# Hybrid retention and attention block: two query splits and two first output loads placed earlier, a key's lower part placed behind the scores

## The chip, the cores and the metric

The kernel runs on 1 core of one Trainium2 chip. The metric is device time in microseconds of one execution. The kernel before took 1036.93 us in the median of 3 runs (1036.6 to 1037.95).

## The reference, cut to what matters

```python
u = rms_norm(h)                                  # 16 learned meta tokens ahead of 1024 positions
rq, rk, rv, rg, aq, ak, av, ag, gr, ga = split(u @ w_in)
o_r = group_norm(bidirectional_retention(rot(rq), rot(rk), rv)) * silu(rg)   # 4 heads
y_r = o_r @ w_ret_branch
o_a = windowed_sink_attention(rot(aq), rot(ak), av) * silu(ag)   # 8 heads, 2 key groups, 128-query blocks
y_a = o_a @ w_attn_branch
mix = sigmoid(gr) * y_r + sigmoid(ga) * y_a
out = h + rms_norm(mix @ w_out)                  # meta rows dropped
```

All of it is float32, with sequence 1024 and width 1024. In one block of the attention, 128 queries see a band of at most 384 keys, 16 meta keys, and a sink logit.

## The kernel before, in words

**Arithmetic.** Each float32 product is made of three passes of TensorE on operands of type float32r (`mm3`, L74 to L79): upper part by upper part (L76), lower by upper (L77), upper by lower (L78). So each operand is first split: the upper part is a rounded copy, made by ScalarE or GpSimd, and the lower part is the rest, a subtraction on VectorE (`dve_lo`, L92). A pass must wait for the part that it reads.

**Stages.** In order of time: projections and retention head by head (to 320 us), the last projection of that kind, the values of the attention (`gen_av`, nine chunks of 128 positions, to 330 us), the attention (to 545 us), and four phases of large products in Strassen's form, z (gates), r and a (branch projections) and o (output), to the end. In the attention and in the phases, TensorE's queue is filled so that some product always stands between a step and the next step that needs its result.

**The attention** goes through 32 chunks (hp, n): hp is a pair of heads, n a block of 128 queries. `stage1` makes the scores (`ps`) by TensorE from the keys `kTh`, `kTl` and the queries `aqh`, `aql`; VectorE adds the mask and takes the maximum (L1447), ScalarE the exponential (L1450), VectorE the reciprocal of its sum (L1454), GpSimd the scaling (`p`, L1463). `stage2` turns the weights by TensorE (`pt`, L1483, L1487, L1488) into two PSUM banks that serve two chunks by turns, and splits them into `pah`/`pal`, `pbh`/`pbl` and `pm`. A chunk's turning therefore needs its own `p` and a bank that `pal` (for L1483) and `pbl` (for L1487) of an earlier chunk have been read out of. `stage3` multiplies them by the values (`po`). Between the stages `fill` issues steps of other work: projections of later queries and keys, and partial products for later phases (`pe`).

The queries of a pair come out of a projection, are rotated (L187, L188 on VectorE, a DMA with addition from GpSimd's queue, L192), and are split by `split_q` into `aqh` (ScalarE, L678) and `aql` (VectorE), each half of the queries and each head of the pair by itself. The keys are split by `keys` into `kTh` (L724) and `kTl`. The table `BEGUN` says at which step of the fillings such a piece of work is issued.

The order on each engine is that of one list for each, made when the program is built; an engine does its list in order and waits at an instruction whose operands aren't there. `tc.issue_after(x)`, and `follow(...)` for several, put what stands inside them behind the instruction x in that order.

**The phases.** A product of a phase waits for its left operand's upper and lower part (`lh`, `ll`) and for its right operand's (`big` and `T`), and adds into a PSUM bank; `combine` reads the banks out (`u3`, `c1`, ...). The right operands of the next phase are loaded or split while the present one runs: `refill` gives the steps as a table of offsets to the end of the phase, `run` hooks them behind the products. For phase o, loaded in phase a, those are: pieces of `w_out` (`a`, L1246, 256 KB each) that are split into `big` (L963 on ScalarE, L92 on VectorE), and sums prepared long before (`preT`, L1142, 1 MB for each of upper and lower part). The left operands of phase o are tiles of the mixed activations, `wro` (512 KB, L1324), read from memory after the branch sums have been added there. All these loads are issued by SyncE in one list, in order.

**The names that the prediction uses:** `val` and `vah`: lower and upper part of the attention's values (L917, L918). `sto0S`, `sto1S`: left operands of phase o that are made from `wro` (L1009). `u3a` (L1077): a sum of phase a that VectorE reads out of the PSUM bank which TensorE's product 3 (`ba` with `lha`, L76) goes on to write.

Of the kernel before, what the change touches and what calls it, by code (L numbers as in the profile page):

```python
# [18 lines left out]
NB = SEQ // P  # L19
# [20 lines left out]
def block_kernel(ctx: ExitStack, tc: tile.TileContext, x0, xT, x, meta, w_in, w_rb, w_ab, w_out, post_w,  # L40
# [629 lines left out]
    def split_q(hp, e_, i):  # L670

        o = aq[hp][e_, i].rearrange("p (t q) -> p t q", q=64)
        if (hp, i) not in aqs:
            aqs[hp, i] = [aw.tile([P, 1024], R, tag=f"aq{t}", bufs=2, name=f"aq{t}{hp}_{i}") for t in "hl"], set()
            if len(aqs) == 1:
                aw.tile([P, 48], F32, name="space_aq")
        h, l = (t.rearrange("p (t e q) -> p t e q", e=2, q=64)[:, :, e_] for t in aqs[hp, i][0])
        nc.scalar.copy(h, o)  # L678
        dve_lo(l, o, h)
        aqs[hp, i][1].add(e_)  # L680


# [31 lines left out]

    rotated_k = {}

    def keys(g, i):

        if not i:
            kT[g] = [ra.tile([P, 4, 272], R, tag="kp", bufs=2, name=f"kT{s}{g}") for s in "hl"]  # L720
        kh, kl = kT[g]
        o = rotated_k.pop((g, i))
        s = NM if i == 0 else 0
        nc.scalar.copy(kh[:, i, 0:256], o[:, s:s + 256])  # L724
        dve_lo(kl[:, i, 0:256], o[:, s:s + 256], kh[:, i, 0:256])
        if i == 0:
            for j in range(4):
                nc.scalar.copy(kh[:, j, 256:272], o[:, 0:NM])
                dve_lo(kl[:, j, 256:272], o[:, 0:NM], kh[:, j, 256:272])
# [173 lines left out]
    def gen_av():  # L903
        w = load_w(w_in, U_AV)
        for c in range(9):
            mt = None if c else vmt
            t = projT(w, c, f"pav{c}", mt)
            if c == 0:
# [5 lines left out]
                for r in range(2):  # L914
                    nc.sync.dma_start(vm[32 * r + NM:32 * r + 2 * NM].bitcast(F32), mt)
            else:
                nc.scalar.activation(vah[:, c - 1], t[:, 0:256], AF.Copy, scale=rcol[:, c:c + 1])  # L917
                nc.vector.scalar_tensor_tensor(low_value(c - 1), t[:, 0:256], rcol[:, c:c + 1],  # L918
# [235 lines left out]
    def refill(nm, src):  # L1154
# [20 lines left out]
        def got(n):  # L1175
            return lambda: get_pre(n)

        def step(at, n, f):
            for k, j in enumerate(n):
                at.setdefault(j, []).append(lambda k=k: f(k))  # L1180

        if nm == "a":
            at = {-16: [load(0, 0)], -14: [load(1, 1)]}
            each(at, -13, split("B11", 0, 0))
            at.update({-11: [got("T1")], -10: [load(1, 0)], -9: [got("T2")], -5: [got("T3")], -1: [got("T4")]})
            each(at, -7, split("B21", 1, 0))
            each(at, -3, split("B22", 1, 1))
            return at

        first = -21 if nm == "z" else -17  # L1190
        at = {first: [load(0, 0), load(0, 1)], -13: [load(1, 1)], -9: [load(1, 0, range(3))]}
        def behind(f):
# [3 lines left out]
            return g  # L1196

        step(at, range(first + 2, first + 6), behind(minus((0, 1), (0, 1), (0, 0))))
        step(at, (-13, -12, -11, -10), split("B11", 0, 0))
# [12 lines left out]
    def run(phases):  # L1212
# [9 lines left out]
        for u in (0, 1):  # L1222
            hooks.setdefault(len(jobs) - len(ph_o.seq) - 11 + u, []).insert(0, lambda u=u: ph_o.block(u, "A11"))
        for k, at in enumerate((16, 27, 46, 58)):
# [98 lines left out]
    def o_load(t, u, j):  # L1323
        nc.sync.dma_start(t, mx_d[4 * j:4 * j + 4, :, 256 * (u ^ 2):256 * (u ^ 2) + 256].rearrange("k p t -> p k t"))  # L1324

# [84 lines left out]
    def attention():  # L1410
# [14 lines left out]
        def stage1(hp, n):  # L1425
# [10 lines left out]
            for x_ in range(2):  # L1436
# [10 lines left out]
                nc.vector.tensor_tensor_reduce(r[:, o:o + wid], s[:, 0:wid], seen, -SCALE,  # L1447
                                               nsink[:, hp:hp + 1], ALU.add, ALU.min, nm_[:, x_:x_ + 1])
# [86 lines left out]
        fill = filler([hooked(works, BEGUN)])[0]  # L1535

        with follow(*latest):
            fill(3)
        with follow(*latest):
            stage1(0, 0)  # L1540
        for k, (hp, n) in enumerate(chunks):
# [28 lines left out]
            if k in (12, 14, 21):  # L1570
# [139 lines left out]
```

## Time and profile before

| | us |
|---|---|
| median of 3 runs | 1036.93 |
| lowest, highest run | 1036.6, 1037.95 |
| the profiled execution, its own time | 1035.83 |
| its span (first to last instruction) | 1034.1 |
| TensorE busy in the span | 1022.3 (99%) |
| VectorE, ScalarE, GpSimd busy | 831.9, 502.0, 226.3 |
| mean granted TensorE clock | 0.998 |

The span is what the trace covers; 1.73 us of the execution's own time lie around it. TensorE is busy through nearly all of the span, so a change of a few microseconds can only be found in the few places where TensorE waits; the view of the waits lists them. In rows of the timeline, the columns are: start in us, duration in us, engine, line, operation, written tile, read tiles, shapes, count, and, in brackets, how long the engine had been idle and what released it. A matmul's duration contains the time it takes to pass through the array, in which the next one already runs: one of 512 columns lasts 0.39 us, and the next starts 0.23 us after it. Idle time of TensorE is therefore shown some 0.16 us shorter than the delay that it makes.

### The profile page before, as it was taken

How to read it: one execution, taken by the hardware profiler on the slowest of the kernel's cores; microseconds unless marked ns; L12 is line 12 of the kernel's file. 1: busy time of each engine (PE TensorE's matmuls, PEld its weight loads, DVE VectorE, ACT ScalarE, POOL GpSimd, SP SyncE). 2: the span in 40 equal slices, each digit the busy share in tenths (PEclk: the TensorE clock that was granted, in tenths of full speed). 3: DMA queues.
4: the chain of work that ended last, by engine and by line, in shares of the span. 5: the costliest groups of instructions: out<-in, count | busy, mean ns of one | idle time of the engine just before them, and what ended most of it. 6: DMA issues, size and time to landing. Idle time of an engine off the chain costs nothing. (4 is left out here: it accounts for less than half of the span.)

```text
span 1034.1 us, 17322 instructions
## 1 busy us (share of the span) xinstructions
PE 1022.3 (99%) x5883; PEld 898.8 (87%) x5883; DVE 831.9 (80%) x1802; ACT 502.0 (49%) x1129; POOL 226.3 (22%) x368
## 2 busy tenths in 40 slices
PE   9999999999999999999999999999999999999997
PEld 8998999989989888988888888888888888887886
DVE  7886759758876787777769999998989899777765
ACT  5531432523423466655667555455567456333442
POOL 3445244243341424443310000000000000110032
PEclk9999999999999999999999999999999999999999
DMA  9433123243241447666559589899874756889563
GB/s 360 164 87 88 63 46 87 76 78 112 80 97 62 103 152 206 184 183 174 154 171 347 178 287 330 312 319 319 276 265 141 257 196 200 246 216 330 139 122 81
DMA packets 98840, 188.45 MB, mean 182 GB/s; under 512 B 13024, under 2 KB 37632, under 8 KB 98192
## 3 DMA queue, kind: packets, MB, share of 16 engines
q1 hardware_dynamic: 81200, 162.89, 46.6%
q0 software_dynamic: 10176, 14.73, 9.5%
q10 hardware_dynamic: 7376, 9.73, 2.8%
q8 instruction: 46, 0.75, 0.3%
q14 instruction: 42, 0.34, 0.1%
HBM read 124.32 MB, written 57.68 MB: 176 GB/s over the span
## 5 line engine op out<-in xcount | busy, mean ns | idle before, releaser
L1310 POOL DMA_DIRECT2D mx_d<-c1a x4 | 3.6, 891 | 395.3 <-DMA a<-in_w_out_dram 368.6
L77 PE MATMUL bz<-big,llz 128*128 128x512 f32 x192 | 74.9, 390 | 0.5 <-DVE llz L92 0.5
L78 PE MATMUL bz<-big,lhz 128*128 128x512 f32 x192 | 74.4, 389 | 0.0
L76 PE MATMUL bz<-big,lhz 128*128 128x512 f32 x192 | 74.1, 389 | 0.0
L76 PE MATMUL pv<-wh,big 128*128 128x256 f32 x256 | 72.9, 285 | 0.0
L77 PE MATMUL pv<-wh,big 128*128 128x256 f32 x256 | 72.8, 284 | 0.0
L78 PE MATMUL pv<-wl,big 128*128 128x256 f32 x256 | 72.7, 284 | 0.0
L78 PE MATMUL bz<-T,lhz 128*128 128x512 f32 x176 | 68.5, 389 | 0.0
L77 PE MATMUL bz<-T,llz 128*128 128x512 f32 x176 | 68.5, 389 | 0.0
L76 PE MATMUL bz<-T,lhz 128*128 128x512 f32 x176 | 68.2, 389 | 0.0
L1450 ACT ACTIVATE p<-raw,nm 128x337 f32<-128x337 f32 (+1 forms) x64 | 35.5, 557 | 34.1 <-DVE nm L1447 30.5
L76 PE MATMUL paq<-big,wh 128*128 128x512 f32 x128 | 51.6, 403 | 0.0
L1463 POOL TENSOR_SCALAR p<-p,den 128x336 f32<-128x336 f32 (+2 forms) x60 | 32.6, 565 | 85.9 <-DVE den L1454 81.1
L78 PE MATMUL paq<-big,wh 128*128 128x512 f32 x128 | 50.2, 392 | 0.0
L77 PE MATMUL paq<-big,wl 128*128 128x512 f32 x128 | 50.2, 392 | 0.0
L76 PEld LDWEIGHTS pv<-wh,big 128*128 128x128 f32 x256 | 48.4, 189 | 0.4
L77 PEld LDWEIGHTS pv<-wh,big 128*128 128x128 f32 x256 | 48.3, 189 | 0.4
L78 PEld LDWEIGHTS pv<-wl,big 128*128 128x128 f32 x256 | 48.3, 189 | 0.3
L92 DVE TENSOR_TENSOR wl<-wr,wh 128x1024 fp32r<-128x1024 f32 x28 | 35.1, 1258 | 11.3 <-POOL wh L89 6.7
L77 PEld LDWEIGHTS bz<-big,llz 128*128 128x128 f32 x192 | 36.1, 188 | 8.1 <-DVE llz L92 0.8
L78 PEld LDWEIGHTS bz<-big,lhz 128*128 128x128 f32 x192 | 36.0, 188 | 7.5
L76 PEld LDWEIGHTS bz<-big,lhz 128*128 128x128 f32 x192 | 36.1, 188 | 7.5
(621 smaller groups left out, 3591.2 us busy)
## 6 DMA issues: line engine op xcount, KB each, us to landing
wrz<-in_w_in_dram SPq DMA_DIRECT2D x32, 512.0 KB, 6.0
wr<-in_w_in_dram SPq DMA_DIRECT2D x29, 512.0 KB, 4.0
we<-in_w_in_dram SPq DMA_DIRECT2D x16, 512.0 KB, 4.2
tg<-tg_d SPq DMA_DIRECT2D x32, 256.0 KB, 5.3
e<-e ACTq DMA_DIRECT2D x20, 256.0 KB, 2.4
e<-e SPq DMA_DIRECT2D x20, 256.0 KB, 4.6
xn<-in_x_dram SPq DMA_DIRECT2D x8, 512.0 KB, 9.4
oTr_d<-ost SPq DMA_DIRECT2D x16, 256.0 KB, 2.1
```

The source lines that it names most:

```text
L76: nc.tensor.matmul(o, ah, bh, start=first, stop=False, **kw)
L77: nc.tensor.matmul(o, al, bh, start=False, stop=False, **kw)
L78: latest[:] = [nc.tensor.matmul(o, ah, bl, start=False, stop=last, **kw).ins]
L92: return nc.vector.tensor_tensor(o, i, hi.bitcast(F32), ALU.subtract).ins
L1310: nc.gpsimd.dma_start(d, to, accum_op=ALU.add)
L1450: last["exp"] = nc.scalar.activation(pp[:, x_, w0 - o:w0 - o + 1 + wid], r[:, 0:1 + wid], AF.Exp, scale=-1.0, bias=nm_[:, x_:x_ + 1], accu ...
L1463: nc.gpsimd.tensor_scalar(v, v, den[:, x_:x_ + 1], 1.0, op0=ALU.mult, op1=ALU.mult)
```

## The change

Four places are changed.

**First queries' splits ahead of the last values.** `gen_av` stops once more, before the read-out of its last chunk, and `split_q` of the first pair's first half (both heads) is issued ahead of it; the last read-out follows the two upper parts. The old place was in `stage1` of the first chunk. On ScalarE, where these are the last read-outs of the values, before:

```order
L917 ACTIVATE vah<-pav_4826,rcol 128x256
L609 ACTIVATE ost_2_4856<-to_2_4853,rnw 128x128 x2
L609 ACTIVATE ost_2_4856<-to_1_4859,rnw 128x128 x2
L917 ACTIVATE vah<-pav_4865,rcol 128x256
L678 CAST aqh_0_4931<-aq_00_4507 128x8x64
L678 CAST aqh_0_4931<-aq_01_4563 128x8x64
```

and after:

```order
L924 ACTIVATE vah<-pav_4826,rcol 128x256
L609 ACTIVATE ost_2_4856<-to_2_4853,rnw 128x128 x2
L609 ACTIVATE ost_2_4856<-to_1_4859,rnw 128x128 x2
L678 CAST aqh_0_4913<-aq_00_4507 128x8x64
L678 CAST aqh_0_4913<-aq_01_4563 128x8x64
L924 ACTIVATE vah<-pav_4865,rcol 128x256
```

The two upper parts of the queries have passed the last chunk's `vah`. On VectorE the last `val` goes, in the same way, from ahead of the preparing memsets and the two `aql` to behind the second `aql`.

**A keys' lower part behind the scores.** `keys(1, 2)` makes the upper part at its old place, and leaves the lower part to the next `stage1`, behind its two score instructions. On VectorE, in chunk (2, 2), before:

```order
L92 TENSOR_TENSOR wl_0_6450<-wr_0_6272,wh_0_6449 128x1024
L92 TENSOR_TENSOR kTl_6223<-akr_2_6374,kTh_6222 128x256
L187 TENSOR_TENSOR m_aq_11_6460<-paq_11_6380,sr 128x512
L188 TENSOR_TENSOR aq_11_6459<-paq_11_6380,cr 128x512
L1447 ISA raw_0_6321,nm_2_6479<-ps_2_0_6481,mask,nsink 128x336
L1447 ISA nm_2_6479 128x1
L1447 ISA raw_1_6329,nm_2_6479<-ps_2_1_6487,mask,nsink 128x336
L1447 ISA nm_2_6479 128x1
L1454 RECIPROCAL den_2_6480<-den_2_6480 128x2
```

and after:

```order
L92 TENSOR_TENSOR wl_0_6449<-wr_0_6272,wh_0_6448 128x1024
L187 TENSOR_TENSOR m_aq_11_6459<-paq_11_6380,sr 128x512
L188 TENSOR_TENSOR aq_11_6458<-paq_11_6380,cr 128x512
L1461 ISA raw_0_6321,nm_2_6478<-ps_2_0_6480,mask,nsink 128x336
L1461 ISA nm_2_6478 128x1
L1461 ISA raw_1_6329,nm_2_6478<-ps_2_1_6486,mask,nsink 128x336
L1461 ISA nm_2_6478 128x1
L92 TENSOR_TENSOR kTl_6223<-akr_2_6374,kTh_6222 128x256
L1471 RECIPROCAL den_2_6479<-den_2_6479 128x2
```

The subtraction `kTl` has gone from ahead of the rotation and the scores to behind them, ahead of the reciprocal.

**A queries' split ahead of a turning.** `split_q(3, 1, 1)` is taken out of the table (step 172) and issued in chunk (3, 2) ahead of `stage2`. On ScalarE `aqh` goes from behind `pah`, `pm`, `pbh` to ahead of them; on VectorE `aql` from behind `pal`, `pm`, `pbl` to ahead of them, right behind the reciprocal.

**First output loads in one row.** The two first `wro` tiles are asked for at one hook (offset -11) ahead of the sums `T1`, which now follow the second of them in SyncE's list; the splits of `w_out`'s pieces are put behind the newest lower part of a left operand. In SyncE's list, before:

```order
L1292 DMA mr_11317<-mx_d 128x512
L1246 DMA a_11347<-in_w_out_dram 128x512
L1324 DMA wro_0_11311<-mx_d 128x4x256
L1142 DMA big_112<-preT_96 128x4x512
L1142 DMA big_113<-preT_97 128x4x512
L1324 DMA wro_0_11339<-mx_d 128x4x256
L1142 DMA T_7800<-preT_98 128x2048
```

and after:

```order
L1305 DMA mr_11319<-mx_d 128x512
L1337 DMA wro_0_11311<-mx_d 128x4x256
L1259 DMA a_11347<-in_w_out_dram 128x512
L1337 DMA wro_0_11313<-mx_d 128x4x256
L1149 DMA big_112<-preT_96 128x4x512
L1149 DMA big_113<-preT_97 128x4x512
L1149 DMA T_7800<-preT_98 128x2048
```

The second `wro` has passed the 2 MB of `preT`, and a last piece of `w_out` now stands behind the first `wro`. On VectorE, `sto1S`, which reads the second `wro`, goes up by two instructions, and some splits of `w_out` change places with neighbours; on TensorE one pass (L77 of `ba`, product 4) goes ahead of twelve passes of product 3.

The diff, cut to its core:

```diff
@@ split_q
-        nc.scalar.copy(h, o)
+        upper = nc.scalar.copy(h, o).ins
         dve_lo(l, o, h)
         aqs[hp, i][1].add(e_)
+        return upper
@@ keys
-    rotated_k = {}
-
-    def keys(g, i):
+    rotated_k, lowers = {}, []
+
+    def keys(g, i, apart=False):
...
-        dve_lo(kl[:, i, 0:256], o[:, s:s + 256], kh[:, i, 0:256])
+        lower = lambda: dve_lo(kl[:, i, 0:256], o[:, s:s + 256], kh[:, i, 0:256])
+        if apart:
+            lowers.append(lower)
+        else:
+            lower()
@@ gen_av
             else:
+                if c == NB:
+                    yield
                 nc.scalar.activation(vah[:, c - 1], t[:, 0:256], AF.Copy, scale=rcol[:, c:c + 1])
@@ refill
+        def got_behind(n):
+            def f():
+                with follow(*asked):
+                    get_pre(n)
+            return f
...
+        def behind(f):
+            def g(k):
+                with tc.issue_after(ahead[0]):
+                    f(k)
+            return g
         if nm == "a":
             at = {-16: [load(0, 0)], -14: [load(1, 1)]}
-            each(at, -13, split("B11", 0, 0))
-            at.update({-11: [got("T1")], -10: [load(1, 0)], -9: [got("T2")], -5: [got("T3")], -1: [got("T4")]})
-            each(at, -7, split("B21", 1, 0))
-            each(at, -3, split("B22", 1, 1))
+            each(at, -13, behind(split("B11", 0, 0)))
+            at.update({-11: [got_behind("T1")], -10: [load(1, 0)], -9: [got("T2")], -5: [got("T3")], -1: [got("T4")]})
+            each(at, -7, behind(split("B21", 1, 0)))
+            each(at, -3, behind(split("B22", 1, 1)))
             return at
@@ run
         for u in (0, 1):
-            hooks.setdefault(len(jobs) - len(ph_o.seq) - 11 + u, []).insert(0, lambda u=u: ph_o.block(u, "A11"))
+            hooks.setdefault(len(jobs) - len(ph_o.seq) - 11, []).insert(u, lambda u=u: ph_o.block(u, "A11"))
@@ o_load
-        nc.sync.dma_start(t, mx_d[4 * j:4 * j + 4, :, 256 * (u ^ 2):256 * (u ^ 2) + 256].rearrange("k p t -> p k t"))
+        asked[:] = [nc.sync.dma_start(
+            t, mx_d[4 * j:4 * j + 4, :, 256 * (u ^ 2):256 * (u ^ 2) + 256].rearrange("k p t -> p k t")).ins]
@@ stage1 of the attention
+            with tc.issue_after(scored):
+                while lowers:
+                    lowers.pop(0)()
             last["sum"] = nc.vector.reciprocal(den, den).ins
@@ the attention's loop
+        with follow(*[split_q(0, e_, 0) for e_ in range(2)]):
+            next(av, None)
         with follow(*latest):
             fill(3)
...
+            if chunks[k] == (3, 2):
+                with follow(*marks("exp", "sum")):
+                    split_q(3, 1, 1)
             with follow(*latest, *marks("exp", "sum")) if not ends else ExitStack():
                 stage2(hp, n)
@@ BEGUN
-             110: [(split_q, 2, 0, 1)], 116: [(keys, 1, 2)], 117: [(half_w, 'q', 3, 0)], 121: [(half_w, 'q', 3, 1)],
+             110: [(split_q, 2, 0, 1)], 116: [(keys, 1, 2, True)], 117: [(half_w, 'q', 3, 0)], 121: [(half_w, 'q', 3, 1)],
...
-             170: [(pre_parts, 11)], 171: [(pre_fetch, 12)], 172: [(split_q, 3, 1, 1)], 176: [(pre_sum, 12, 0)],
+             170: [(pre_parts, 11)], 171: [(pre_fetch, 12)], 176: [(pre_sum, 12, 0)],
```

More of the change, by code (lines that the diff above doesn't have):

```diff
@@ L1180, in step @@
                 at.setdefault(j, []).append(lambda k=k: f(k))
-        if nm == "a":
-            at = {-16: [load(0, 0)], -14: [load(1, 1)]}
-            each(at, -13, split("B11", 0, 0))
-            at.update({-11: [got("T1")], -10: [load(1, 0)], -9: [got("T2")], -5: [got("T3")], -1: [got("T4")]})
-            each(at, -7, split("B21", 1, 0))
-            each(at, -3, split("B22", 1, 1))
-            return at
-        first = -21 if nm == "z" else -17
-        at = {first: [load(0, 0), load(0, 1)], -13: [load(1, 1)], -9: [load(1, 0, range(3))]}
         def behind(f):
@@ L1196, in behind @@
             return g
+        if nm == "a":
+            at = {-16: [load(0, 0)], -14: [load(1, 1)]}
+            each(at, -13, behind(split("B11", 0, 0)))
+            at.update({-11: [got_behind("T1")], -10: [load(1, 0)], -9: [got("T2")], -5: [got("T3")], -1: [got("T4")]})
+            each(at, -7, behind(split("B21", 1, 0)))
+            each(at, -3, behind(split("B22", 1, 1)))
+            return at
+        first = -21 if nm == "z" else -17
+        at = {first: [load(0, 0), load(0, 1)], -13: [load(1, 1)], -9: [load(1, 0, range(3))]}
         step(at, range(first + 2, first + 6), behind(minus((0, 1), (0, 1), (0, 0))))
@@ L1446, in stage1 @@
                 o, w0 = (0, 64) if x_ else (1, 1)
-                nc.vector.tensor_tensor_reduce(r[:, o:o + wid], s[:, 0:wid], seen, -SCALE,
-                                               nsink[:, hp:hp + 1], ALU.add, ALU.min, nm_[:, x_:x_ + 1])
+                scored = nc.vector.tensor_tensor_reduce(r[:, o:o + wid], s[:, 0:wid], seen, -SCALE,
+                                                        nsink[:, hp:hp + 1], ALU.add, ALU.min, nm_[:, x_:x_ + 1]).ins
                 last["exp"] = nc.scalar.activation(pp[:, x_, w0 - o:w0 - o + 1 + wid], r[:, 0:1 + wid], AF.Exp,
```

## The prediction, made before the changed kernel had run

> **What bounds the kernel now.** I read the view of TensorE's waits first, since the page has TensorE busy in 99% of the span: a change can win only where TensorE stands still, and lose by making it stand still elsewhere.
>
> ```profile
> PE ps L77 <- DVE aql L92: 1.0, 2, 0.5
> PE ba L76 <- DVE u3a L1077: 0.6, 1, 0.6
> PE pt L1483 <- DVE pal L92: 0.5, 1, 0.5
> PE bz L77 <- DVE llz L92: 0.5, 1, 0.5
> PE pt L1487 <- DVE pbl L92: 0.4, 1, 0.4
> PE pt L1483 <- POOL p L1463: 0.2, 1, 0.2
> ```
>
> The columns are total, count and longest, in us. These are seven waits (but for the first matmul of the kernel), six of them for VectorE. The change touches five: both of the first row (places 1 and 3), the third and fifth (place 2), the second (place 4). It leaves the fourth and sixth alone. I then went through the timeline at each place.
>
> **Place 1, the first scores.**
>
> ```profile
> 327.11 1.14 ACT L609 ACTIVATE ost<-to,rnw 128x128 f32<-128x128 f32 x4
> ...
> 329.92 0.47 ACT L917 ACTIVATE vah<-pav,rcol 128x256 fp32r<-128x256 f32 x1 [1.68 <-PE pav L78]
> ...
> 330.30 1.13 ACT L678 CAST aqh<-aq 128x512 fp32r<-128x512 f32 x2
> ...
> 331.78 0.41 PE L76 MATMUL ps<-kTh,aqh 128*128 128x272 f32 x2
> ...
> 331.96 0.68 DVE L92 TENSOR_TENSOR aql<-aq,aqh 128x512 fp32r<-128x512 f32 x1
> 332.70 0.39 PE L77 MATMUL ps<-kTh,aql 128*128 128x272 f32 x1 [0.51 <-DVE aql L92]
> 332.93 0.29 PE L78 MATMUL ps<-kTl,aqh 128*128 128x272 f32 x1
> ```
>
> ScalarE stands idle 1.68 us, up to 329.92, with the two `aqh` queued behind the last `vah`. In the new order they start when `ost` ends, at 327.11 + 1.14 = 328.25, and end at 329.38, before `vah` can start; so `vah` loses nothing. Both `aql`, 0.68 each, can then be done by about 329.38 + 0.7 = 330.1 to 330.8 (the short memsets ahead of them fill VectorE's idle time). TensorE asks for them at 331.78 + 2 x 0.13 = 332.03 (a pass of 272 columns takes 0.13), so some 1.2 us are in hand, and the wait of 332.70 - 332.03 = 0.67 goes. The next pass starts 0.23 after the delayed one and not 0.13: a wait costs 0.10 more behind it. The last `val`, moved behind the `aql`, is still ready some 0.5 us ahead of the first score's masking, which is in turn behind TensorE. Sum of the place: **0.77**.
>
> **Place 2, the key's lower part.**
>
> ```profile
> 452.43 0.42 DVE L92 TENSOR_TENSOR kTl<-akr,kTh 128x256 fp32r<-128x256 f32 x1 [0.88 <-ACT kTh L724]
> ...
> 454.07 0.56 DVE L1447 CUSTOM_DVE_ANT_0 raw<-ps,mask,nsink 128x336 f32<-128x336 f32 x1
> ...
> 456.47 0.69 DVE L92 TENSOR_TENSOR pal<-pt,pah 128x512 fp32r<-128x512 f32 x1 [0.30 <-ACT pah L1493]
> 456.51 0.32 PE L78 MATMUL ps<-kTl,aqh 128*128 128x336 f32 x1
> ...
> 457.30 0.71 PE L1483 MATMUL pt<-ident,p 128*128 128x128 f32 x4 [0.47 <-DVE pal L92]
> ...
> 457.87 0.42 DVE L92 TENSOR_TENSOR pbl<-pt,pbh 128x256 fp32r<-128x256 f32 x1
> ...
> 458.44 0.41 PE L1487 MATMUL pt<-ident,p 128*128 128x128 f32 x2 [0.42 <-DVE pbl L92]
> ```
>
> VectorE stands idle for 0.88 because `kTl` waits for `kTh`, which itself waits for the rotated key; the rotation and the two scores queue behind it. With `kTl` gone, they start 0.88 earlier and have 0.42 less ahead of them: the first score moves by 1.30, from 454.07 to 452.77. Its exponential, the reciprocal, `pah`, `pal` and `pbl` hang on it in a chain, so `pal` ends at 457.16 - 1.30 = 455.86, and `pbl` at 458.29 - 1.30 = 456.99. `kTl` itself falls into VectorE's idle time between the scores and the reciprocal, and its reader, the next chunk's third pass, comes after 456. TensorE reaches the turning at 456.51 + 0.15 = 456.66, so its first wait, 0.64, goes. It reaches L1487 four passes of 0.11 later, at 457.10; `pbl` plus the 0.15 from its end to TensorE's start (458.29 to 458.44) gives 457.14. Of the second wait, 458.44 less 457.86 (four passes, the first of them 0.22 in the trace's pace behind a wait) = 0.58, about 0.04 stays. Sum: **1.2**. Some 0.1 may come on top at the sixth wait above, 8 us later: its releaser hangs on VectorE, which moves by 1.30, where TensorE moves by 1.2.
>
> **Place 3, the last queries' split.**
>
> ```profile
> 514.25 1.07 POOL L1463 TENSOR_SCALAR p<-p,den 128x336 f32<-128x336 f32 x2 [4.70 <-PE pe L78]
> 514.38 0.69 DVE L92 TENSOR_TENSOR pal<-pt,pah 128x512 fp32r<-128x512 f32 x1 [0.31 <-ACT pah L1493]
> ...
> 515.04 0.62 ACT L678 CAST aqh<-aq 128x512 fp32r<-128x512 f32 x1
> ...
> 515.86 0.47 PE L76 MATMUL ps<-kTh,aqh 128*128 128x336 f32 x2
> ...
> 516.12 0.68 DVE L92 TENSOR_TENSOR aql<-aq,aqh 128x512 fp32r<-128x512 f32 x1
> ...
> 516.85 0.42 PE L77 MATMUL ps<-kTh,aql 128*128 128x336 f32 x1 [0.53 <-DVE aql L92]
> ...
> 518.01 0.38 PE L1487 MATMUL pt<-ident,p 128*128 128x128 f32 x2
> ```
>
> `aqh` takes `pah`'s place on ScalarE: it runs from about 513.8 to 514.4, `aql` from 514.43 to 515.11. TensorE needs it at 515.86 + 2 x 0.15 = 516.17: the wait of 0.68 and the 0.11 behind it go, 0.79. The price is that `pal` starts not at 514.38 but about 515.04, and `pbl` ends 0.66 later, at 516.85 (in the old order it ends at 516.19, where `aql` starts). TensorE, earlier by 0.79, reaches L1487 at 518.01 - 0.79 = 517.22: some 0.2 to 0.3 in hand. But `aql` now runs beside GpSimd's `p`, and the trace shows what a subtraction with both inputs in SBUF does beside GpSimd:
>
> ```profile
> 114.80 0.62 POOL L89 TENSOR_SCALAR qh<-qr 128x512 fp32r<-128x512 f32 x1
> ...
> 114.86 0.82 DVE L92 TENSOR_TENSOR Slf<-Sf,Shf 128x256 fp32r<-128x256 f32 x1
> ...
> L92 DVE TENSOR_TENSOR Slf<-Sf,Shf x32: 407/416/1262, 47.1 to 291.6; 128x256 fp32r<-128x256 f32 x32
> ```
>
> Begun 0.06 behind GpSimd, it took 0.82 where its median is 0.416, and ended 0.26 behind GpSimd's end. If `aql` gets its turn between the two `p` (the first ends at about 514.80), it ends near 515.34, `pbl` near 517.08, and the margin is used up but not passed: I take **0.75**, bounds 0.79 and 0.2 (rival A).
> The Trainium skill, "SBUF — State Buffer", section "Who interferes with whom", says that a VectorE instruction with two SBUF inputs and a GpSimd instruction that reads SBUF exclude each other, the later one blocked until the earlier ends; by that rule the subtraction is blocked here, and the row at 114.86 agrees (0.82 against 0.416).
>
> **Place 4, the first output loads.**
>
> ```profile
> 916.92 0.33 SPq L1246 DMA_DIRECT2D a<-in_w_out_dram  x1
> 922.78 0.38 SPq L1324 DMA_DIRECT2D wro<-mx_d  x1
> ...
> 924.63 0.57 SPq L1324 DMA_DIRECT2D wro<-mx_d  x1
> ...
> DMA to landing us min/median/max: 3.2/4.1/11.0
> ...
> 935.76 0.69 DVE L1009 TENSOR_TENSOR sto1S<-wro 128x512 f32<-128x512 f32 x1 [4.18 <-DMA wro<-mx_d]
> ...
> 941.79 0.68 DVE L1077 TENSOR_TENSOR u3a<-u3a,ba 128x512 f32<-128x512 f32 x1
> ...
> 942.52 0.51 PE L76 MATMUL ba<-big,lha 128*128 128x512 f32 x1 [0.56 <-DVE u3a L1077]
> ```
>
> The row on landing is that of all `wro` loads. The second one, issued at 924.63 behind 2 MB of sums, is the one that took 11.0; VectorE stood 4.18 us for it, and everything up to `u3a` came late. The wait is 0.56 by the row and 0.16 more that the modelled end of the matmul in front hides, with 0.1 behind it: 0.82. In the new order the load goes out behind the first `wro` and one 256 KB piece, about 0.4 each, so at 923.6. Landing after 3.2 to 4.1, as its like do: 926.8 to 927.7; with the slowest, 11.0: 934.6. From `sto1S` to the end of `u3a` it is 942.47 - 935.76 = 6.71 in the old order, and no more in the new one; TensorE asks at 942.52 - 0.72 = 941.80. So any landing before 935.1 frees it. I take the whole, **0.82**; the other end is nothing, if 11.4 us or more pass.
>
> **Sum.** 0.77 + 1.2 + 0.1 + 0.75 + 0.82 = 3.6. The profiled execution's own time is 1035.83, its span 1034.1; it would become 1032.2, the span 1030.5. The median shown, 1036.93, is 1.1 above that execution, so the forecast is 1036.93 - 3.6 = **1033.3**. About 0.2% (2.1 us) is what a measurement of this kernel can tell from no change.
>
> **The rivals.**
> A. At place 3, `aql` gets no turn between the two `p`, and starts only after 515.32: it ends near 515.86, `pbl` near 517.60, and TensorE's L1487 waits to 517.7 instead of 517.22, 0.5 and 0.1 behind it. For it: the row at 114.86. Against: `p` is two instructions. Time 1033.9.
> B. Place 4 does nothing, because the second `wro` still takes over 11.4 us. For it: the one of 11.0. Against: that one had 2 MB ahead. Time 1034.1.
> C. What TensorE wins ahead of phase z is taken back there, because a transfer doesn't move along:
>
> ```profile
> 538.64 0.80 SPq L1241 DMA_DIRECT2D wrz<-in_w_in_dram  x2
> ...
> 544.32 0.69 DVE L1025 TENSOR_TENSOR stz0S<-wrz,wrz 128x512 f32<-128x512 f32 x1 [3.66 <-DMA wrz<-in_w_in_dram]
> ```
>
> Phase z's first weights land 5.7 us after their issue, and the fourth wait above hangs on them. Were 544.32 fixed in time, the 2.8 of places 1 to 3 would be waited away, and only place 4's 0.82 stay: 1036.1. Against it: the issue waits for a VectorE step of the chunk before, which moves with TensorE.
> D. Slower than before: SyncE now stands at the first `wro` until 922.78 with the last piece of `w_out` behind it, which went out at 916.92. Its split stands ahead of `u3a` on VectorE, in both orders. From the piece's landing to `u3a`'s end it takes ScalarE's copy and three instructions of VectorE, about 2.6; TensorE asks at 941.80. A landing past 939.2 delays TensorE by as much, and one past 942, near 19 us after the issue, eats the 2.8 of the other places; at 944 the time is 1039. Against it: the slowest load above took 11.0.
>
> **How the numbers follow.** Forecast 0.62, A 0.14, B 0.07, C 0.11, D 0.06. Forecast, A and B are faster by more than 0.2%: 0.83; C is within: 0.11; D is slower: 0.06. The range, 1032.4 to 1034.6, takes in A, B and, below, the 0.2 that the sixth wait and place 2 can still give, with the 0.3 to 1.0 by which runs of one kernel differ.
>
> **What would show it.** In the changed kernel's waits of TensorE, the rows `ps <- aql`, `pt <- pal`, `pt <- pbl` and `ba <- u3a` are gone, and `bz <- llz` keeps 0.5. VectorE's 4.18 before `sto1S` is below 1. `aql` near 514 lasts longer than 0.68. A row `pt L1487 <- pbl` near 515 speaks for A, `bz <- llz` above 2 for C, a wait of ScalarE for `a` near 930 for D. The prediction is wrong if those rows are gone and the span is still above 1032.

## The result, and the profile after

The changed kernel takes **1033.9 us** (median of 21 runs, 1032.3 to 1035.79), the kernel before, run beside it, 1036.26 (21 runs, 1034.0 to 1037.95). The ratio is 0.9981, with a 95% interval of 0.9975 to 0.9988: a gain of 2.0 us, between 1.2 and 2.6. The forecast was a gain of 3.6, to 1033.3. The direction and the range held, but just over half of the gain came. (The three runs known before the forecast had their median at 1036.93, 0.67 above that of the 21, which brings the time nearer to the forecast than the gain.) The profiled execution of the changed kernel took 1033.5, its span is 1031.7 where the old one was 1034.1.

TensorE's waits after the change, total, count and longest in us:

```profile
PE idle L322 <- DVE warm L216: 1.4, 1, 1.4
PE pe L77 <- DVE wel L92: 0.6, 1, 0.6
PE pq L76 <- ACT big L342: 0.3, 1, 0.3
PE pt L1500 <- POOL p L1480: 0.2, 1, 0.2
PE bz L77 <- DVE llz L92: 0.2, 1, 0.2
```

The rows `aql`, `pal`, `pbl` and `u3a` are gone, as forecast. (Delays below some 0.3 get no row: of the wait for `pbl`, 0.27 is left at place 2, and 0.23 stands at place 3. The row `pq <- big`, from the kernel's first microseconds, stood in the view before too, with 0.2.) But a row has come that did not exist before: `pe <- wel`, the lower part of a gate's weights, some 9 us behind place 3. That is the wait that took place 3's gain, as the experiments below show.

**Place 1** in the timeline of the changed kernel:

```profile
328.42 1.17 ACT L678 CAST aqh<-aq 128x512 fp32r<-128x512 f32 x2
...
329.93 0.68 DVE L92 TENSOR_TENSOR aql<-aq,aqh 128x512 fp32r<-128x512 f32 x1
330.24 0.47 ACT L924 ACTIVATE vah<-pav,rcol 128x256 fp32r<-128x256 f32 x1 [0.65 <-PE pav L78]
...
332.35 0.29 PE L77 MATMUL ps<-kTh,aql 128*128 128x272 f32 x1
```

Both `aql` are done by 330.61, `vah` waits only for TensorE, and the pass on `aql` starts without a wait.

**Place 2:**

```profile
452.56 0.56 DVE L1461 CUSTOM_DVE_ANT_0 raw<-ps,mask,nsink 128x336 f32<-128x336 f32 x1
...
453.53 0.42 DVE L92 TENSOR_TENSOR kTl<-akr,kTh 128x256 fp32r<-128x256 f32 x1
...
456.38 0.42 DVE L92 TENSOR_TENSOR pbl<-pt,pbh 128x256 fp32r<-128x256 f32 x1
...
456.95 0.41 PE L1504 MATMUL pt<-ident,p 128*128 128x128 f32 x2
```

`kTl` lies behind the scores, as planned. The first score moved from 454.07 to 452.56 (the split of weights ahead of it was 0.22 earlier too), the wait for `pal` is gone, and of that for `pbl` 0.27 is left.

**Place 3, and what follows it.** Four rows behind place 3 in the kernel before, which the waits of TensorE don't point to:

```profile
517.38 0.69 DVE L813 TENSOR_TENSOR we<-we,we 128x512 f32<-128x512 f32 x1 [0.58 <-DMA we<-in_w_in_dram]
517.99 0.56 DVE L1447 CUSTOM_DVE_ANT_0 raw<-ps,mask,nsink 128x336 f32<-128x336 f32 x1
...
524.92 1.23 DVE L92 TENSOR_TENSOR wel<-we,weh 128x1024 fp32r<-128x1024 f32 x1
...
526.25 0.45 PE L77 MATMUL pe<-big,wel 128*128 128x512 f32 x1
```

and the changed kernel:

```profile
512.63 0.61 ACT L678 CAST aqh<-aq 128x512 fp32r<-128x512 f32 x1
513.10 1.50 POOL L1480 TENSOR_SCALAR p<-p,den 128x336 f32<-128x336 f32 x2 [4.69 <-DVE den L1471]
513.27 0.91 DVE L92 TENSOR_TENSOR aql<-aq,aqh 128x512 fp32r<-128x512 f32 x1 [0.34 <-ACT aqh L678]
...
515.41 0.42 DVE L92 TENSOR_TENSOR pbl<-pt,pbh 128x256 fp32r<-128x256 f32 x1
...
516.20 0.69 DVE L818 TENSOR_TENSOR we<-we,we 128x512 f32<-128x512 f32 x1 [0.36 <-DMA we<-in_w_in_dram]
516.80 0.56 DVE L1461 CUSTOM_DVE_ANT_0 raw<-ps,mask,nsink 128x336 f32<-128x336 f32 x1
...
523.75 1.23 DVE L92 TENSOR_TENSOR wel<-we,weh 128x1024 fp32r<-128x1024 f32 x1
...
525.03 0.50 PE L77 MATMUL pe<-big,wel 128*128 128x512 f32 x1 [0.61 <-DVE wel L92]
```

`aql` lasts 0.91 and GpSimd's two `p` 1.50 (1.07 in the old order): they get in each other's way, and by as much as the middle case had it (514.43 to 515.34, 0.91). Its wait is gone. But look at what stands behind on VectorE: the first of three sums on the raw gate weights, `we`, waits for its transfer, and the two scores of the next chunk stand behind it in the same row. Between the kernel before and this one, `we` moved from 517.38 to 516.20 and `wel` from 524.92 to 523.75, by 1.18 and 1.17; TensorE had moved by 1.99 there. So TensorE now arrives at `wel` 0.78 too early. The transfer itself hangs on VectorE: in both profiles SyncE issues its first half 0.03 us after VectorE's earlier sum of the same kind has ended, at 510.70 before and at 509.55 now, so that it moved by 1.15.

**Place 4:**

```profile
921.69 0.37 SPq L1337 DMA_DIRECT2D wro<-mx_d  x1
...
926.20 0.69 DVE L1016 TENSOR_TENSOR sto1S<-wro 128x512 f32<-128x512 f32 x1 [0.38 <-DMA wro<-mx_d]
...
935.56 0.69 DVE L1084 TENSOR_TENSOR u3a<-u3a,ba 128x512 f32<-128x512 f32 x1
```

The second load lands 4.5 after its issue, VectorE's wait ahead of `sto1S` fell from 4.18 to 0.38, and `u3a` ends at 936.25, some 4 us before TensorE asks for it (941.80 in the old order, less the 1.46 won by then).

**How the stretches are compared.** TensorE's order is the same in all kernels here up to near 545 and almost the same behind, so the n-th matmul of two traces is the same matmul, and the difference of its two starts tells how far one execution is ahead at that place. The table has this difference against the first profile of the kernel before, in us (minus is earlier): first as it stands at 331, then how it changes over a stretch. The other stretches change it by less than 0.3, but for e8, which lost 3.33 between 460 and 500, and for 530 to 546, where e8 gained 0.48 and e12 0.47.

| execution | at 331 | place 1 (331-336) | place 2 (450-460) | 500-530 | 331-530 in all | 546-930 | place 4 (930-950) | at the end |
|---|---|---|---|---|---|---|---|---|
| before, once more (e7) | +0.28 | +0.02 | -0.63 | +0.12 | -0.44 | +0.93 | -0.24 | +0.25 |
| changed | +0.31 | -0.78 | -1.09 | +0.28 | -1.51 | +0.03 | -0.89 | -2.36 |
| changed, once more (e10) | +0.17 | -0.78 | -1.37 | +0.75 | -1.42 | +0.30 | -0.89 | -1.89 |
| all but place 3 (e1) | +0.15 | -0.78 | -1.30 | +0.79 | -1.24 | +0.70 | -0.89 | -1.38 |
| place 3 alone (e2) | +0.47 | +0.02 | -0.87 | +0.65 | +0.04 | +1.40 | -0.89 | +0.88 |
| place 2 alone (e4) | +0.08 | -0.01 | -1.22 | +0.75 | -0.32 | +2.79 | -0.89 | +1.38 |
| place 1 alone (e5) | +0.10 | -0.78 | +0.28 | +0.14 | -0.28 | +5.30 | -0.89 | +4.10 |
| place 4 alone (e6) | +0.19 | +0.01 | -1.07 | +0.44 | -0.58 | +1.29 | -0.89 | +0.03 |
| sum behind the scores (e3) | -0.22 | -0.78 | -0.94 | -0.87 | -2.55 | +1.06 | -0.89 | -2.79 |
| the same, once more (e11) | +0.03 | -0.78 | -1.37 | -0.87 | -3.07 | +0.80 | -0.89 | -3.33 |
| e3, first llz ahead (e12) | +0.26 | -0.78 | -1.24 | -0.43 | -2.16 | +1.80 | -0.89 | -1.47 |
| e3 without place 3 (e9) | +0.15 | -0.78 | -1.30 | +0.43 | -1.89 | +0.65 | -0.89 | -2.19 |
| e3 and two more edits (e8) | +0.50 | -0.78 | -1.30 | -0.60 | +0.65 | +0.41 | -0.89 | +0.19 |

Read down a column, three things stand out. Place 1 gives 0.78 whenever it is in and nothing otherwise. Place 2's column is negative also where place 2 is not in (e7, e2, e6): the same code loses less time there in other executions. And place 4's column is -0.89 also where place 4 is not in (e2, e4, e5). So the forecast's prices at both places were those of one execution. At place 2 that was one in which the rotated key came late (e7 below), at place 4 one in which TensorE came early (e6 below).

### The profile page after: what moved, and what is told of

Its sections match the earlier page's. It is cut to its first block, busy times and chain, and to the rows that moved or that the text cites. A ratio compares the mean times of both kernels' runs of the same rounds, so it can differ in the third digit from the quotient of the medians.

```text
span 1031.7 us, 17320 instructions
## 1 busy us (share of the span) xinstructions
PE 1021.9 (99%) x5883; PEld 899.0 (87%) x5883; DVE 832.9 (81%) x1802; ACT 502.0 (49%) x1129; POOL 226.6 (22%) x368
## 5 line engine op out<-in xcount | busy, mean ns | idle before, releaser
L77 PE MATMUL bz<-big,llz 128*128 128x512 f32 x192 | 74.8, 390 | 0.2 <-DVE llz L92 0.2
L77 PE MATMUL pv<-wh,big 128*128 128x256 f32 x256 | 72.7, 284 | 0.0
L77 PE MATMUL bz<-T,llz 128*128 128x512 f32 x176 | 68.5, 389 | 0.0
L77 PE MATMUL paq<-big,wl 128*128 128x512 f32 x128 | 50.2, 392 | 0.0
L77 PEld LDWEIGHTS pv<-wh,big 128*128 128x128 f32 x256 | 48.3, 189 | 0.4
L92 DVE TENSOR_TENSOR wl<-wr,wh 128x1024 fp32r<-128x1024 f32 x28 | 35.2, 1259 | 10.3 <-POOL wh L89 6.7
L77 PEld LDWEIGHTS bz<-big,llz 128*128 128x128 f32 x192 | 36.0, 188 | 7.9 <-DVE llz L92 0.5
```

Of the source, the lines that this page charges most:

```text
L77: nc.tensor.matmul(o, al, bh, start=False, stop=False, **kw)
L92: return nc.vector.tensor_tensor(o, i, hi.bitcast(F32), ALU.subtract).ins
```

## The experiments

The theories: **T**, VectorE's row behind 500 hangs on the transfers of the gates' weights, and TensorE can't be further ahead than `wel` lets it. **L**, each wait removed is kept. **S**, the wait for `wel` is the price of place 3's later `pal` and `pbl`. Later **V**: what a wait on a transfer costs differs from one execution to the next.

**e1, the changed kernel with place 3 undone.**

```
-            if chunks[k] == (3, 2):
-                with follow(*marks("exp", "sum")):
-                    split_q(3, 1, 1)
-             170: [(pre_parts, 11)], 171: [(pre_fetch, 12)], 176: [(pre_sum, 12, 0)],
+             170: [(pre_parts, 11)], 171: [(pre_fetch, 12)], 172: [(split_q, 3, 1, 1)], 176: [(pre_sum, 12, 0)],
```

> The changed kernel with place 3 undone: the split of the last queries stands again where it stood before. Theory T (VectorE's row from 503 us on hangs on the gate weights' transfers, which moved by only 1.15 us; TensorE can't get further ahead of it than wel allows): TensorE waits 1.1 to 1.3 for aql near 516, and no more than 0.1 for wel near 525; behind 530 it stands within 0.1 of where it stands in the changed kernel, and the time is the changed kernel's within 0.5. Theory L (each wait removed is kept; what place 3 won stays won): behind 530 TensorE is 0.5 to 0.75 later than in the changed kernel. Theory S (the wait for wel is the price of place 3's later pal and pbl on VectorE): the wait for aql is 0.7, there is none for wel, and behind 530 TensorE is 0.3 earlier than in the changed kernel.

1034.33 us (11 runs), ratio to the kernel before 0.9985 (0.9976 to 0.9993), beside 0.9981 with place 3. The timeline of e1:

```profile
515.52 0.43 PE L77 MATMUL ps<-kTh,aql 128*128 128x336 f32 x1 [0.56 <-DVE aql L92]
...
516.30 0.69 DVE L818 TENSOR_TENSOR we<-we,we 128x512 f32<-128x512 f32 x1 [0.84 <-DMA we<-in_w_in_dram]
...
523.85 1.23 DVE L92 TENSOR_TENSOR wel<-we,weh 128x1024 fp32r<-128x1024 f32 x1
...
525.13 0.50 PE L77 MATMUL pe<-big,wel 128*128 128x512 f32 x1
```

TensorE loses 0.72 to `aql` and 0.22 at the score's first pass ahead of it (less in one place than T said, 1.1 to 1.3), and still 0.22 to `wel`, for which S had none and T no more than 0.1. `wel` starts at 523.85 with the old order of place 3 and at 523.75 with the new one, so S falls: `wel` isn't late because of place 3. Behind 530 TensorE is 0.11 later than in the changed kernel by the start of the same matmul (0.27 counted from 331), not the 0.5 to 0.75 of L.

**e2, place 3 alone.** The edit of e1 the other way round, on the kernel before.

> The kernel before with place 3 alone. T: the wait for aql near 516 falls from 0.68 to 0.2 or less, and a wait of 0.4 to 0.7 for wel appears near 525, since wel ended in the kernel before just as TensorE asked for it; behind 530 TensorE stands within 0.2 of the kernel before, and the time is within 0.3 of it. L: the 0.5 to 0.75 stays behind 530 and in the time.

1036.98 us (11 runs), ratio 1.0007 (0.9998 to 1.0016): nothing is won. The wait for `aql` is gone, `pbl` takes 0.27, and `wel` 1.00, more than the 0.4 to 0.7 expected:

```profile
517.88 0.69 DVE L813 TENSOR_TENSOR we<-we,we 128x512 f32<-128x512 f32 x1 [0.58 <-DMA we<-in_w_in_dram]
...
525.43 1.23 DVE L92 TENSOR_TENSOR wel<-we,weh 128x1024 fp32r<-128x1024 f32 x1
...
526.71 0.50 PE L77 MATMUL pe<-big,wel 128*128 128x512 f32 x1 [0.76 <-DVE wel L92]
```

Behind 530 TensorE is 0.51 later than in the first profile of before (expected: within 0.2), because in this execution the transfer was issued 0.31 later and landed 0.50 later. L falls.

**e3, the changed kernel with the waiting sum behind the scores.**

```
+    def sum_behind(u, i):
+        lowers.append(lambda: pre_sum(u, i))
...
-176: [(pre_sum, 12, 0)],
+176: [(sum_behind, 12, 0)],
```

> The changed kernel, and the first sum of the last but one gate's weights, which waits for its transfer until 516.2 with the two scores queued behind it on VectorE, stands behind these scores. T: the two scores start about 0.9 earlier (near 515.9), the wait for wel near 525 falls from 0.78 to 0.15 or less, behind 530 TensorE is 0.6 to 0.8 earlier than in the changed kernel; of this the start of phase z (bz for llz) can take back up to 0.3, so the time is 0.4 to 0.8 less than the changed kernel's. S: the wait for wel stays at 0.6 or more, since pal and pbl stay as late as they are; the time is that of the changed kernel.

1033.32 us (11 runs), ratio 0.9978 (0.9967 to 0.9988). VectorE in e3:

```profile
514.77 0.57 DVE L1464 CUSTOM_DVE_ANT_0 raw<-ps,mask,nsink 128x336 f32<-128x336 f32 x1
515.27 0.56 DVE L1464 CUSTOM_DVE_ANT_0 raw<-ps,mask,nsink 128x336 f32<-128x336 f32 x1
...
515.75 0.69 DVE L818 TENSOR_TENSOR we<-we,we 128x512 f32<-128x512 f32 x1
...
521.89 1.22 DVE L92 TENSOR_TENSOR wel<-we,weh 128x1024 fp32r<-128x1024 f32 x1
```

The scores start at 514.77 and not 516.80, and `wel` at 521.89 and not 523.75. There is no wait for `wel`; between 500 and 530 TensorE gains 0.87 where the changed kernel lost 0.28. At phase z's start it waits 0.44 for `llz` instead of 0.33. T's rows came, S's did not. Behind 530 TensorE is 1.57 earlier than in the changed kernel, more than T's 0.6 to 0.8; 0.42 of that it had already at 500.

**e4, place 2 alone.**

```
+        if apart:
+            lowers.append(lower)
...
+            with tc.issue_after(scored):
+                while lowers:
+                    lowers.pop(0)()
...
-116: [(keys, 1, 2)]
+116: [(keys, 1, 2, True)]
```

> The kernel before with place 2 alone. T (place 2 gave 1.09 and not 1.2 to 1.3 because the weights' split wl ahead of the rotation hangs on a transfer that moved by 0.22 where place 1 had moved TensorE by 0.42): without place 1 the second wait, for pbl, is 0.1 or less, and TensorE is 1.2 to 1.3 earlier past 460. Theory R (taking kTl out of the row is worth less than the 1.30 worked out): the wait for pbl is 0.27 again, and TensorE 1.0 to 1.1 earlier past 460. Both: the wait for aql near 516 is 0.7 to 1.1, since VectorE's row there moves less than TensorE.

1035.21 us (11 runs), ratio 0.9995 (0.9986 to 1.0004): by the times not to be told from no change. Both waits of place 2 are gone, and TensorE gains 1.22 there, as T had it. But T's reason doesn't stand: it made place 1 responsible for the 0.27 that the changed kernel kept, and e1, which has place 1, waits for nothing at place 2. It was that execution. Between 500 and 530 e4 loses 0.75 of what it won.

**e5, place 1 alone.** `gen_av` with `if c == NB: yield`, `split_q` that returns its upper part, and

```
+        with follow(*[split_q(0, e_, 0) for e_ in range(2)]):
+            next(av, None)
```

> The kernel before with place 1 alone. Both theories: the wait for aql near 332 is gone and TensorE is 0.78 earlier behind it. T (TensorE can't stay ahead of VectorE's row, whose gate weights' transfers don't follow): the waits at place 2, near 516 and 525 grow, and at the start of phase z 0.1 to 0.4 of the 0.78 is left. L (each removed wait is kept): 0.7 to 0.8 is left there and in the time.

1035.49 us (11 runs), ratio 0.9991 (0.9982 to 1.0). 0.78 is won at place 1, and at place 2 0.28 is lost again: its waits have grown to 0.87 and 0.59 (0.64 and 0.59 in the first profile). Those near 516 and 525, which T had growing too, are 0.72 and none. Behind 530, 0.28 is left, and 0.40 at phase z's start, the upper edge of T's 0.1 to 0.4; but the unchanged kernel in e7 stands at -0.44 there, so one profile can't settle this.

**e6, place 4 alone.**

```
-            hooks.setdefault(len(jobs) - len(ph_o.seq) - 11 + u, []).insert(0, lambda u=u: ph_o.block(u, "A11"))
+            hooks.setdefault(len(jobs) - len(ph_o.seq) - 11, []).insert(u, lambda u=u: ph_o.block(u, "A11"))
...
-        nc.sync.dma_start(
+        asked[:] = [nc.sync.dma_start(
...
+                with follow(*asked):
+                    get_pre(n)
```

> The kernel before with place 4 alone. Both: VectorE's wait ahead of sto1S is below 1 us and u3a ends well ahead of TensorE's ba. Theory V (the late landing that place 4 was priced by is one execution's: in e2 and e4, which lack place 4, TensorE did not wait for u3a either): the time is that of the kernel before within 0.5. L: 0.8 to 0.9 less than the kernel before.

1035.78 us (11 runs), ratio 0.9998 (0.999 to 1.0007). VectorE waits 0.59 ahead of `sto1S`, TensorE none for `u3a`, and the time is within 0.5 of the kernel before, as V had it. The interval reaches to a gain of 1.0, so the times alone don't exclude L's 0.8. V's reason does not stand, either: without place 4 the second `wro` was late in all five executions (before, e7, e2, e4, e5), 10.3 to 11.6 from its issue to the start of `sto1S`; with place 4 it took 4.5 to 5.8 (changed, e10, e6, e3). In e2:

```profile
925.97 0.58 SPq L1324 DMA_DIRECT2D wro<-mx_d  x1
...
936.59 0.69 DVE L1009 TENSOR_TENSOR sto1S<-wro 128x512 f32<-128x512 f32 x1 [3.23 <-DMA wro<-mx_d]
...
942.61 0.68 DVE L1077 TENSOR_TENSOR u3a<-u3a,ba 128x512 f32<-128x512 f32 x1
```

`u3a` ends there 0.82 later than in the first profile, but TensorE comes 1.77 later and finds it done. What differs between the executions is how late TensorE itself arrives.

**e7, the kernel before, unchanged.**

> The kernel before, unchanged, profiled once more, to see which of its waits every execution has. V (the waits whose releaser hangs on a transfer differ from one execution to the next by as much as they are long): the wait for aql near 332 and the one for POOL's p near 465 are there within 0.05; those at place 2 (1.22 together in the first profile), at 942 (0.72) and at phase z's start (0.62) differ by over 0.2, at least two of the three; another wait for llz near 757 or 790 of 0.5 to 1.0 may stand. L: each of these waits is there within 0.1 of the first profile.

Ratio 0.9999 (0.999 to 1.0007). The wait for `aql` near 332 is 0.67 in both profiles, that for `p` 0.40 and 0.39. Place 2's are 0.59 in all, not 1.22; place 4's 0.48, not 0.72; that of phase z 0.34, not 0.62; and one of 0.80 for `llz` stands at 790, which the first profile did not have. All of V's points came. What varies at place 2 is the arrival of the rotated key. One row from e2, two from e5, all with place 2's code as it was before:

```profile
452.28 0.42 DVE L92 TENSOR_TENSOR kTl<-akr,kTh 128x256 fp32r<-128x256 f32 x1
```

```profile
451.67 0.41 ACT L725 CAST kTh<-akr 128x256 fp32r<-128x256 f32 x1 [2.06 <-DMA akr<-m_ak]
452.10 0.43 DVE L92 TENSOR_TENSOR kTl<-akr,kTh 128x256 fp32r<-128x256 f32 x1 [1.24 <-ACT kTh L725]
```

In the first profile VectorE stood idle for 0.88 ahead of `kTl`; in e2 not at all, in e6 not at all, in e7 0.43, in e5 1.24. Place 2's two waits of TensorE follow it: 1.23, 0.46, 0.29, 0.59, 1.46.

**e8, two more waits.** e3, and `BEHIND = "aq1_10", "aq3_10", "ak1_3"`, so that GpSimd issues a key's rotation behind the scaling `p`; and at phase z's start

```
+                with follow(*self.first):
                     g(t, t, self.block(u, "A11"), sub)
```

> e3 with two more edits: the rotation of the last keys' piece (ak1_3) is issued by GpSimd behind the scaling p that it stands ahead of near 461, and at phase z's start the first llz stands ahead of the second subtraction of stz0S on VectorE. Both theories: the wait for p near 463 (0.40) is gone, 0.4 to 0.5 with what stands behind it. T with e3's edit in: wel has 0.4 in hand near 525, so no wait or up to 0.2 comes back there; the wait for llz at phase z's start falls from 0.44 to 0.2 or less; behind 550 TensorE is 0.5 to 0.8 earlier than in e3, the time 0.3 to 1.0 less than e3's.

1036.53 us (11 runs), ratio 1.0007 (0.9999 to 1.0016): both theories were wrong, by over 3 us. The wait for `p` is gone, but the rotation went out not behind this `p` but behind the next chunk's, 6 us later, and the key's upper part waited for it in ScalarE's row:

```profile
466.99 1.68 POOL L192 DMA_DIRECT2D akr<-m_ak  x2 [0.18 <-issue]
...
470.84 0.40 ACT L725 CAST kTh<-akr 128x256 fp32r<-128x256 f32 x1 [1.13 <-DMA akr<-m_ak]
471.28 0.43 DVE L92 TENSOR_TENSOR kTl<-akr,kTh 128x256 fp32r<-128x256 f32 x1 [1.56 <-ACT kTh L725]
471.30 0.42 PE L76 MATMUL ps<-kTh,aqh 128*128 128x336 f32 x1 [2.00 <-ACT kTh L725]
```

TensorE waited 2.16 us, and then ran slower for some 4 us (below).

**e9, e3 with place 3 undone** (the edits of e1 and e3 together).

> e3 (the first sum of the gate's weights behind the scores) with place 3 undone. T (place 3 was worth nothing only because wel set TensorE's time behind it; e3 has lifted that): TensorE waits 0.7 to 1.3 for aql near 516, not for wel near 525; from 500 to 530 it loses 0.5 to 0.8 more than in e3, where it gained 0.87 against the kernel before. Rival N (place 3 moves a wait to somewhere else in any case, by GpSimd and VectorE getting in each other's way): from 500 to 530 the two are alike within 0.2.

1034.85 us (11 runs), ratio 0.999 (0.998 to 1.0), beside 0.9973 for e3's kernel in the same stretch of runs. The wait for `aql` is 0.72, with 0.20 at the score's first pass, and none for `wel`. From 500 to 530 it loses 1.30 more than e3 and 0.86 more than e12, somewhat over T's 0.5 to 0.8, and not N's 0.2. So place 3's gain is kept once `wel` doesn't set the time.

**e10, the changed kernel once more; e11, e3 once more; e12, e3 with the second edit of e8 alone.**

> The changed kernel, unchanged, profiled once more. T: wel ends 7.5 to 7.6 plus its own 1.2 behind the start of the first sum near 516, and TensorE behind 530 stands where wel's end puts it, as in the eight profiles so far without e3's edit (within 0.1); the wait for wel is 0.3 to 1.0. L: no wait for wel. Of the waits that hang on transfers, one for llz near 757 or 790 can stand in this execution.

> e3 once more, beside the changed kernel on the same chip. T: no wait for wel, the lead from 500 to 530 is 0.7 to 1.0 against the kernel before, and over the runs the time is 0.3 to 1.0 less than that of the changed kernel beside it. S: the same time as the changed kernel within 0.2.

> e3 with the second edit of e8 alone: at phase z's start the first llz stands ahead of the second subtraction of stz0S. T: the wait for llz near 543 falls from 0.44 to 0.2 or less, and a wait of 0.3 for lhz some 10 us later, as e8 had it, takes it back: behind 560 TensorE is within 0.15 of e3's place. L: 0.25 to 0.3 is kept.

| kernel | median, us | runs | ratio to before | 95% interval |
|---|---|---|---|---|
| changed (e10) | 1034.02 | 11 | 0.9988 | 0.9979 to 0.9997 |
| e3 again (e11) | 1033.22 | 7 | 0.9973 | 0.9962 to 0.9983 |
| e12 | 1033.28 | 11 | 0.9975 | 0.9966 to 0.9984 |
| before, beside them | 1035.72 | 29 | | |

e10 waits 0.95 for `wel`, so the new wait is no accident of one execution. e11 has none, and is 0.80 us under the changed kernel beside it, within T's 0.3 to 1.0; e3 alone, with intervals this wide, could not have told that. (The means of those 11 and 7 runs differ by 1.5, with a 95% interval of 0.8 to 2.3.) In e12 the wait for `llz` falls to 0.15, and one of 0.29 comes 10 us later, as T said; behind 560 its profile is 1.0 behind e3's and not within 0.15, but 0.87 of that it was at 530 already. e3's kernel, from which e12 can't be told apart by the times, is the fastest version here: 2.5 to 2.8 us under the kernel before by the medians.

The position of TensorE against `wel`, in the nine executions without e3's edit (us):

| execution | first sum `we` starts | `wel` starts | the matmul near 530 starts | `wel` less `we` | that matmul less `wel` |
|---|---|---|---|---|---|
| before | 517.38 | 524.92 | 530.11 | 7.54 | 5.19 |
| e7 | 517.25 | 524.80 | 529.95 | 7.55 | 5.15 |
| e5 | 517.22 | 524.77 | 529.92 | 7.55 | 5.15 |
| e6 | 516.97 | 524.52 | 529.72 | 7.55 | 5.20 |
| e4 | 517.16 | 524.71 | 529.87 | 7.55 | 5.16 |
| e2 | 517.88 | 525.43 | 530.62 | 7.55 | 5.19 |
| e1 | 516.30 | 523.85 | 529.01 | 7.55 | 5.16 |
| changed | 516.20 | 523.75 | 528.90 | 7.55 | 5.15 |
| e10 | 516.13 | 523.69 | 528.85 | 7.56 | 5.16 |

Whatever was changed ahead of it, TensorE stands 5.15 to 5.20 behind the start of `wel`, and `wel` 7.55 behind the sum that waits for the transfer. TensorE's pass that reads `wel` starts 0.05 to 0.06 after `wel` has ended in eight of the nine, and 0.11 after in the first profile, where `wel` came just in time. With e3's edit the last column is 5.3 to 5.5 and that distance 0.32 to 0.44, so TensorE is no longer tied to it. This table together with e3 and e9, which take the tie away, shows T.

## Why the forecast was right in sign and too large

**Place 1, 0.77: right.** 0.78 in all nine executions that have it.

**Place 2, 1.2 and 0.1: the mechanism right, the size one execution's.** The step that failed is "With `kTl` gone, they start 0.88 earlier and have 0.42 less ahead of them". The 0.42 is the kernel's, the 0.88 is an arrival: it was 0, 0, 0.43, 0.88 and 1.24 in five executions. TensorE's two waits are 0.81 on average in these five, and 0.07 in the nine with place 2 (0.27, 0.33 and seven times none). So about 0.7 to 0.8 is the place's worth (the table's column has 1.24 on average with place 2, and 0.46, from -0.28 to 1.07, without). The extra 0.1 at the sixth wait did not come: 0.39 before and after.

**Place 3, 0.75: wrong.** Its local part was worked out well (`aql` 0.91, the wait gone, and of rival A's 0.6 for `pbl` only 0.23 to 0.27). The failed step is the sum's silent one, that a wait which goes at 516 is time won at the end. The forecast priced `bz <- llz` at phase z's start as the place where a transfer could take it back (rival C) and held against it that the transfer's issue moves with TensorE. It did not look 9 us behind place 3, where `wel` in the profile of before ended at 524.92 + 1.23 = 526.15 just as TensorE asked for it: without a wait, so no row in the view of waits, but also without anything in hand. Rival C's mechanism was the right one, at another transfer and for place 3's part only: e1, e2 and e9 show it.

**Place 4, 0.82: the mechanism right, the size one execution's.** The load itself is late in every execution of the old order, and early with the edit (e6). But TensorE's loss there without the edit was 0.89, 0.65 and three times nothing. The step that failed is "I take the whole": it took TensorE's arrival at 941.80 for the kernel's. The two executions that wait are those in which TensorE was least late at 930 (0 and 0.49 against the first profile); the three without a wait were 1.77, 2.28 and 4.99 late, and `sto1S`, which waits for the load, only 0.83, 0.80 and 3.37. On average about 0.3. In the changed kernel TensorE is 1.0 to 1.5 early at 930, so there the old order may cost more than that; no run has places 1 to 3 without place 4, and its worth in the changed kernel stays open. Rival D did not come: no row shows ScalarE waiting for `a`.

**The sum.** By the places, with place 4 at its average, 0.8 + 0.8 + 0 + 0.3 = 1.9. By TensorE's position behind 530, which is what counts with T: the three executions with the old code up to there (before, e7, e6) stand at 0, -0.44 and -0.58, the two of the changed kernel at -1.51 and -1.42, a gain of 1.1, and 0.3 for place 4, 1.4. Both lie in the measured 1.2 to 2.6. Places 1 and 2 alone brought 0.9 and 0.5 by the times, with intervals of 0.9 either way; how much of each survives by itself stays open. That 1033.9 lies in the range is in part luck: the range was as wide as that for rivals A and B, neither of which came as described (of A's 0.6 there were 0.23), and not for what took place 3's gain. By the prediction's own sign, those rows gone and the span still above 1032, the profiled 1031.7 stays just below it; the second profile of the changed kernel (e10) has 1032.2, and the median run's span is 1032.1.

## What to carry to other kernels

A wait that goes is a gain only as far as the next step that has nothing in hand, and that step may have no row in the view of waits: before a gain is summed, follow the waiting engine on, and read for each operand when it ended and when it was asked for. In an engine that works in order, an instruction that waits for a transfer belongs behind those that could go already; moving one sum behind two scores was worth as much as place 3 had promised. And a price read from one execution, where a transfer or the arrival of the waiting engine sets it, is one draw: profile the unchanged kernel more than once before summing waits of half a microsecond.

## What the runs showed of the hardware

In e8 and e5, a long wait slowed TensorE beyond its own length. The granted clock (PEclk, the third column from the right) of e8 around its wait of 2.16 us, which ended at 471.30:

```profile
466.00:470.00 4.00, 3.30 (x20) 2.74 (x18) 3.58 (x8) 0.64 (x2) 3.08 (x7) 1.00 0.52 124
471.00:474.00 3.00, 2.70 (x12) 2.65 (x13) 1.49 (x5) 0.77 (x3) 0.06 (x1) 0.61 0.89 221
474.00:477.00 3.00, 3.00 (x14) 2.47 (x13) 1.82 (x6) 1.96 (x8) 1.44 (x4) 0.82 0.21 36
477.00:480.00 3.00, 3.00 (x20) 2.67 (x19) 2.29 (x5) 1.05 (x1) 0.07 (x1) 1.00 0.00 0
```

e5 waited 1.57 up to 759.30, with 0.50 more up to 760.03, and 1.25 up to 637.87:

```profile
762.00:764.50 2.50, 2.50 (x8) 2.00 (x7) 2.50 (x5) 0.89 (x2) 0.00 (x0) 0.60 1.05 392
...
637.80:640.00 2.20, 2.13 (x9) 1.76 (x10) 2.20 (x5) 1.55 (x4) 0.00 (x0) 1.00 1.04 404
```

Behind the pair the clock fell to 0.60, behind the single wait it stayed at 1.00. So the wait of 1.25 cost its length and 0.2; that of 2.16 cost 3.8 by the same matmul's start at 470 and 500, and the 2.07 of the pair cost 3.9 by its start at 757 and 766.
The Trainium skill, "TensorE: Matmul & The Clock Gate", section "What's actually happening", has a half-rate clock after at least one idle window of about 3.4 us; here a wait of 2.16, and two of 2.07 together, were enough, so the measurement decides.

Between 546 and 930 nearly the same code lost 0.03 to 5.30 us more than in the first profile, mostly in waits of phase z near 635, 757 and 790 that come and go, where VectorE or ScalarE waits for transfers (the 5.30 of e5 has some 1.8 from the lower clock in it). The difference at 331 spread over 0.7. Together they are enough for the 4 us by which the runs of one kernel differ.
